# The second half of eight weight-row subtractions on GpSimd instead of VectorE, in a decoder layer on one core

## The chip, the cores and the metric

The kernel runs on one core of a Trainium2 chip. A core has TensorE (PE in the rows; PEld is its weight load), VectorE (DVE), ScalarE (ACT), GpSimd (POOL) and SyncE (SP), and 16 DMA engines; each compute engine works off its own queue in order, and the queues wait for each other through semaphores. The metric is the device time of the whole program in microseconds, measured without a profiler, as the median over runs.

## The reference

One decoder layer on 256 tokens of width 2048. What matters here is its beginning:

```python
c_act = jax.nn.silu(c)
mod = (c_act @ w_ada[l] + b_ada[l]).reshape(B, 6, 1, D)
shift1, scale1, gate1, shift2, scale2, gate2 = jnp.moveaxis(mod, 1, 0)
h = rmsnorm(x, g_norm_mix[l]) * (1.0 + scale1) + shift1
q_a, k_c, v_c, k_s, v_s, k_w, v_w, g_a, q_r, k_r, v_r, g_r = split_cols(h @ w_in[l], IN_SIZES)
...
x = x + gate1 * (jnp.concatenate([o_nsa, o_ret], axis=-1) @ w_out[l])
h2 = rmsnorm(x, g_norm_ffn[l]) * (1.0 + scale2) + shift2
x = x + gate2 * peer_ffn(h2, peer_w_q[l], peer_sub_keys[l], peer_u[l], peer_v[l])
```

The first projection `h @ w_in` feeds sparse attention and retention; the layer ends with a retrieval over 16384 single-neuron experts, whose two matrices of 128 MB each are streamed in whole.

## The kernel before, in words

Weights stay in float32. For a product at nearly float32 accuracy, a weight row is split into a high part `hi`, rounded to a narrower float32 form (`fp32r`) that TensorE takes, and a low part `lo = raw - hi`; activations are split in the same way into `hh` and `hl` (both in the tile `act`). A product is then three matmuls: hi·hh, hi·hl, lo·hh. `split_to` makes the two parts in two halves of the row: for each half a ScalarE copy (L157) makes `whi`, and a VectorE subtraction (L158) makes `wlo`.

The first projection runs in stages. Stage A, the one that the change touches, goes over `KH` = 8 rows of `winA`, k = 0 to 7, one row being the 128 inputs of block k by 2048 outputs. For each row:

- `win_row` loads 1 MB into one of four `raw` buffers (L348) and calls `split`.
- `row_in(k)` first makes two `ada_chunk`s per row: each loads a 1 MB row of `w_ada` into a `raw` buffer (L148) and multiplies and sums it against silu(c) with one VectorE `scalar_tensor_tensor` of 128x2048 (L198), whose sum is one column of scale1 or shift1. Two small VectorE operations (L338, L339) make `scol`, the scale of block k. Then `modulate` scales the block on ScalarE (L295, which needs `scol`), rounds it to `hh` on ScalarE (L296), and subtracts to `hl` on VectorE (L297).
- 48 matmuls of 128x256 (L354) go into the eight PSUM banks `bkA0` to `bkA7`.

So each row asks for 3 MB of DMA, and for two L158, two L198 and one L297 on VectorE. SyncE issues the loads in program order; a load waits until the buffer that it takes is free: of the three loads for block k+2, the first takes the buffer of `winA` row k, and so waits for both L158 of row k, and the next two take the buffers of the `ada` rows of block k+1, and wait for its two L198.

Ahead of the loop VectorE normalises the input with four products of 128x1024 (L300), after ScalarE has copied the row of inverse norms (`rrow`, L275); a 128x2 power on GpSimd (L221) stands in that chain. After the loop the eight banks are copied to `oT`, four on ScalarE (L372) and four on VectorE (L370), and stage C starts on `winC` with four of the banks.

The order on each engine is not that of the source: a list scheduler, which works with estimated durations, decides it when the program is built. Only loads and operations that are pinned keep the written order, and none in stage A is.

Of the kernel before, what the change touches and what calls it, by code (L numbers as in the profile page):

```python
# [9 lines left out]
F32 = mybir.dt.float32  # L10
# [105 lines left out]
def body(ctx, tc, a, out, dbg=None, stop=None):  # L116
    nc = tc.nc
# [15 lines left out]
    def chunk_tile(name, dt, tag=None):  # L133
        pool, bufs = strm[-1]
        return pool.tile([P, 2048], dt, name=name, tag=tag or name, bufs=bufs[tag or name])

    def raw_tile():
        if not ring:
            return chunk_tile("raw", F32)
        t = min(ring, key=lambda t: (ring[t][1] + 1) / ring[t][0])  # L140
        ring[t][1] += 1
        if t == "more":
            return ring[t][2].tile([P, 2048], F32, name="raw", tag="more", bufs=2)
        return chunk_tile("raw", F32, t)

    def load(src):
        r = raw_tile()
        i = nc.sync.dma_start(r, src)  # L148
        if ring:
            tc.keep_in_program_order(i)  # L150
        return r

    def split_to(r, hi, lo, parts=1):
        n = hi.shape[-1] // parts
        for i in range(parts):
            sl = slice(i * n, i * n + n)
            nc.scalar.copy(hi[:, sl], r[:, sl])  # L157
            nc.vector.tensor_sub(lo[:, sl], r[:, sl], hi[:, sl].bitcast(F32))  # L158

    def split(r, n=2048, parts=2):  # L160
        hi, lo = chunk_tile("whi", F32R)[:, 0:n], chunk_tile("wlo", F32R)[:, 0:n]
        split_to(r[:, 0:n], hi, lo, parts)
        return hi, lo


# [62 lines left out]
    def t_blocks(pool, src_chunks, tags=("A", "A"), parts=2, dst=None):  # L228

        if dst:  # L230
            split_to(load(src_chunks[0]), *dst, parts)
        w = [dst] if dst else [split(load(c), parts=parts) for c in src_chunks]
        ps = [pool.tile([P, 2, S], F32, name="psA", tag=t) for _, t in zip(w, tags)]
        for k in range(KB):
            sl = slice(k * P, (k + 1) * P)
            for p_, (hi, lo) in zip(ps, w):
                nc.tensor.matmul(p_, hi[:, sl], act[:, k], start=k == 0, stop=False, skip_group_check=True)  # L237
                nc.tensor.matmul(p_[:, 1, :], lo[:, sl], hh[:, k, :], start=False, stop=k == KB - 1, skip_group_check=True)  # L238
        return ps
# [39 lines left out]
    with ExitStack() as fctx:  # L279
# [48 lines left out]
        def background(n=1):  # L328
            credit[0] += PACE[n] if isinstance(n, str) else n
            n = int(credit[0] + 1e-6)  # L330
            credit[0] -= n
            for _ in range(n):
                if not todo:
                    return
                j, k = todo.pop(0)
                ada_chunk(j, k, crow)
                if j == 0:
                    nc.vector.tensor_add(modc[:, 0:2, k], modc[:, 0:2, k], b_col[:, 0:2, k])  # L338
                    nc.vector.tensor_scalar(scol[:, 0, k:k + 1], modc[:, 1, k:k + 1], 1.0, g_mix[:, k:k + 1],  # L339
                                            op0=OP.add, op1=OP.mult)  # L340
                elif 1 < j < 5 and k == KB - 1:
                    nc.vector.tensor_add(modc[:, j, :], modc[:, j, :], b_col[:, j, :])
                    if j == 4:
                        nc.vector.scalar_tensor_tensor(scol[:, 1, :], modc[:, 4, :], 1.0, g_ffn, op0=OP.add, op1=OP.mult)

        def win_row(src, k, n):
            r = raw_tile()
            nc.sync.dma_start(r[:, 0:n], src[k])  # L348
            return split(r, n)

        def rows_T(bank, b, hi, lo, col, k, k0, k1, first=True):
            w = slice(col, col + P)
            for n, (x, y) in enumerate(((hi, hh), (hi, hl), (lo, hh))):
                nc.tensor.matmul(bank[:, b, :], x[:, w], y[:, k, :], start=k == k0 and n == 0 and first,  # L354
                                 stop=k == k1 - 1 and n == 2, skip_group_check=True)
# [6 lines left out]
        def row_in(k):  # L362
            while len(todo) > 80 + LATE - 2 * (k + 1):
                background(1)
            modulate(k, k + 1, xT[:, k:k + 1, :], 0, 0, hh, hl)
# [8 lines left out]
        background(2)  # L374
        bk = banks("bkA", [P, 2, S], "AASSTTOO")
        for k in range(KH):
            hi, lo = win_row(a["winA"], k, 2048)
            row_in(k)
            background("A")
            for b in range(16):  # L380
                rows_T(bk[b // 2], b % 2, hi, lo, b * P, k, 0, KH, b % 2 == 0)
        wait_in(oT, bk)
        bk = banks("bkC", [P, 2, S], "AASS")
        for q in range(KH // 2):
            hi, lo = split(load(a["winC"][q].rearrange("p k e -> p (k e)")))
            background("C")
            for k in (2 * q, 2 * q + 1):
                for b in range(8):
                    rows_T(bk[b // 2], b % 2, hi, lo, (k % 2) * 1024 + b * P, k, 0, KH, b % 2 == 0)
# [4 lines left out]
        for k in range(KB):  # L394
            hi, lo = win_row(a["winB"], k, NB)
            if k >= KH:
                row_in(k)
            if len(todo) > 46 + LATE:
                background("B")
            for b in range(8):  # L400
                rows_T(bk[b // 2], b % 2, hi, lo, b * P, k, 0, KB, b % 2 == 0)
            for tt in range(2):
                ts_ = slice(tt * P, (tt + 1) * P)
                w = slice(8 * P, 8 * P + 512)
                for n, (x, y) in enumerate(((hh, hi), (hh, lo), (hl, hi))):
                    nc.tensor.matmul(bv[tt], x[:, k, ts_], y[:, w], start=k == 0 and n == 0,  # L406
                                     stop=k == KB - 1 and n == 2)
            rows_T(bg, 0, hi, lo, 8 * P + 512, k, 0, KB)
# [67 lines left out]
        for kv in range(2):  # L476
# [9 lines left out]
            for pb in range(16):  # L486
                i = nc.tensor.matmul(psc, w1[:, pb * P:(pb + 1) * P], blk[:, pb], start=pb == 0, stop=pb == 15)
# [34 lines left out]
        for gp in range(2):  # L522
# [91 lines left out]
            for q in range(2):  # L614
                src = []
# [89 lines left out]
        for q in range(4):  # L705
            sl = slice(q * 512, (q + 1) * 512)
# [20 lines left out]
        for q in range(4):  # L727
            sl = slice(q * 512, (q + 1) * 512)
# [613 lines left out]
def build(tc, a, out, dbg=None):  # L1342
    with ExitStack() as ctx:
        body(ctx, tc, a, out, dbg)
# [17 lines left out]
```

## Time and profile before

| what | value |
|---|---|
| median of 3 runs | 1859.46 us (1855.84 to 1864.89) |
| the profiled execution, its own time | 1856.91 us |
| its span | 1855.2 us |
| PE busy | 1793.1 us (97%) |
| VectorE busy | 1485.7 us (80%) |
| ScalarE busy | 708.7 us (38%) |
| GpSimd busy | 366.1 us (20%) |
| DMA | 653.96 MB, mean 353 GB/s |

Busy shares are means over the whole span. The stage that the change touches is the first 90 us, and what bounds the kernel there is read from rows of that stretch. Times in rows count from the start of the span.

### The profile page before, as it was taken

Reading aid. Unit: us, or ns where it says so; the run is one execution under the profiler, and the core shown is the slowest. Engines: PE = TensorE matmul, PEld = TensorE weight load, DVE = VectorE, ACT = ScalarE, POOL = GpSimd, SP = SyncE. Lnnn points to the kernel's source line nnn. Section 1 sums busy time; section 2 is a strip of 40 time slices with the busy share of each in tenths; the row PEclk is TensorE's granted clock in tenths of the full one; section 3 lists DMA queues with packets and bytes.
Section 4 is the critical chain, followed back from the end, with each engine's and each line's share of the span. In section 5 each row is a group of like instructions: output and inputs, shape, how many; then the busy total and the mean of one; then the engine's idle time right before and its main releaser. Section 6 shows DMA issues by size and latency. Waiting matters only on the chain.

```text
span 1855.2 us, 28510 instructions
## 1 busy us (share of the span) xinstructions
PE 1793.1 (97%) x11264; PEld 1571.5 (85%) x11264; DVE 1485.7 (80%) x2336; ACT 708.7 (38%) x1284; POOL 366.1 (20%) x259
## 2 busy tenths in 40 slices
PE   5899999999889999999999999999999999999997
PEld 4899878797767899999997777779999998777775
DVE  7988889889779999586498999983555558998878
ACT  3444453745435421021045555541111114555554
POOL 1000001011010012211124434420111114544210
PEclk9999899999999999999999999999999999999999
DMA  8989887889887799999889999989999989999992
GB/s 341 409 320 362 313 308 292 342 302 334 318 338 279 278 322 364 424 366 376 332 346 386 423 420 416 409 355 425 367 345 359 354 316 404 426 421 403 388 316 99
DMA packets 94616, 653.96 MB, mean 353 GB/s; under 512 B 11409, under 2 KB 11633, under 8 KB 18449
## 3 DMA queue, kind: packets, MB, share of 16 engines
q1 hardware_dynamic: 66818, 467.78, 65.2%
q0 software_dynamic: 27664, 184.37, 25.3%
q8 instruction: 88, 1.44, 0.3%
q14 instruction: 46, 0.38, 0.1%
HBM read 644.97 MB, written 4.22 MB: 350 GB/s over the span
## 4 chain that ended last, share of the span: by engine, by line
PE 87%; DVE 7%; DMA 3%; issue 1%; ACT 1%; POOL 0%; SPq 0%; ACTq 0%; POOLq 0%; DVEq 0%
PE acc L990 31%; PE psU L1111 28%; PE psN L453 8%; PE psD L354 4%; PE psA L237 3%; PE bkB L354 2%; DMA raw<-in_adaT 2%; PE psA L238 1%; PE pg L1096 1%; DVE raw L198 1%; DVE wlo L158 1%; PE bkC L354 1%; PE bvB L406 1%; DMA raw<-in_winA 1%; PE pT L552 1%
## 5 line engine op out<-in xcount | busy, mean ns | idle before, releaser
L1111 PE MATMUL psU<-xT,raw 128*128 128x160 f32 x4096 | 569.5, 300 | 0.0
L1111 PEld LDWEIGHTS psU<-xT,raw 128*128 128x128 f32 x4096 | 558.3, 190 | 0.4
L990 PE MATMUL acc<-whi,cc 128*128 128x512 f32 x1512 | 369.1, 391 | 0.0
L990 PEld LDWEIGHTS acc<-whi,cc 128*128 128x128 f32 x1512 | 283.8, 188 | 70.0 <-issue 1.5
L967 DVE TENSOR_TENSOR wlo<-raw,whi 128x2048 fp32r<-128x2048 f32 x126 | 288.1, 2287 | 55.1 <-issue 47.4
L990 PE MATMUL acc<-wlo,cc 128*128 128x512 f32 x1008 | 254.2, 392 | 0.8 <-DVE wlo L967 0.6
L964 ACT CAST whi<-raw 128x2048 fp32r<-128x2048 f32 x126 | 240.7, 1911 | 0.5 <-DMA raw<-in_v 0.5
L198 DVE SCALAR_TENSOR_TENSOR raw<-raw,crow 128x2048 f32<-128x2048 f32 x96 | 219.0, 2283 | 19.7 <-DMA raw<-in_adaT 19.6
L157 ACT CAST whi<-raw 128x1024 fp32r<-128x1024 f32 (+1 forms) x174 | 168.5, 1018 | 167.1 <-DMA raw<-in_winA 32.4
L158 DVE TENSOR_TENSOR wlo<-raw,whi 128x1024 fp32r<-128x1024 f32 (+1 forms) x174 | 200.6, 1181 | 24.2 <-ACT whi L157 23.8
L990 PEld LDWEIGHTS acc<-wlo,cc 128*128 128x128 f32 x1008 | 161.5, 161 | 63.8 <-DVE wlo L967 3.1
L453 PE MATMUL psN<-whi,act 128*128 128x512 f32 x512 | 166.9, 402 | 1.4 <-ACT act L677 0.7
L1117 DVE TENSOR_TENSOR X<-X,ge 128x160 f32<-128x160 f32 (+19 forms) x94 | 25.8, 276 | 162.7 <-ACT ge L1116 160.5
L1113 ACT ACTIVATE X<-psU 128x160 f32<-128x160 f32 (+19 forms) x102 | 25.6, 251 | 315.6 <-PE psU L1111 299.6
L453 PEld LDWEIGHTS psN<-whi,act 128*128 128x128 f32 x512 | 95.9, 189 | 25.6 <-issue 1.7
L453 PE MATMUL psN<-wlo,act 128*128 128x512 f32 x256 | 103.3, 404 | 3.4 <-DVE wlo L158 3.4
L953 ACT CAST cc<-X 128x192 fp32r<-128x192 f32 x126 | 44.0, 352 | 148.1 <-PE acc L990 147.5
L237 PE MATMUL psA<-act,whi 128*128 128x512 f32 x240 | 87.2, 404 | 3.8 <-ACT whi L157 3.8
L806 POOL DMA_INDIRECT rows<-in_urow,sx x32 | 67.1, 2097 | 105.3 <-DVE rows L847 100.4
L806 POOL DMA_INDIRECT s<-in_urow,sx x26 | 53.9, 2072 | 120.6 <-DVE s L847 86.5
L354 PE MATMUL psD<-act,whi 128*128 128x256 f32 x384 | 75.4, 294 | 0.6 <-ACT whi L157 0.6
L969 ACT CAST cc<-cc 128x64 fp32r<-128x64 f32 x126 | 30.4, 243 | 117.2 <-DVE cc L954 117.2
(363 smaller groups left out, 2551.0 us busy)
## 6 DMA issues: line engine op xcount, KB each, us to landing
raw<-in_u SPq DMA_DIRECT2D x128, 1024.0 KB
raw<-in_v SPq DMA_DIRECT2D x128, 1024.0 KB
raw<-in_adaT SPq DMA_DIRECT2D x96, 1024.0 KB
raw<-in_winN SPq DMA_DIRECT2D x16, 1024.0 KB
raw<-in_woutN SPq DMA_DIRECT2D x16, 1024.0 KB
raw<-in_wqT SPq DMA_DIRECT2D x16, 1024.0 KB
raw<-in_winB SPq DMA_DIRECT2D x16, 832.0 KB
raw<-in_winD SPq DMA_DIRECT2D x12, 1024.0 KB
```

The lines of the kernel that those rows point to most:

```text
L157: nc.scalar.copy(hi[:, sl], r[:, sl])
L158: nc.vector.tensor_sub(lo[:, sl], r[:, sl], hi[:, sl].bitcast(F32))
L198: nc.vector.scalar_tensor_tensor(r, r, 1.0, crow, op0=OP.mult, op1=OP.mult, accum_out=modc[:, j, k:k + 1])
L237: nc.tensor.matmul(p_, hi[:, sl], act[:, k], start=k == 0, stop=False, skip_group_check=True)
L354: nc.tensor.matmul(bank[:, b, :], x[:, w], y[:, k, :], start=k == k0 and n == 0 and first, stop=k == k1 - 1 and n == 2, skip_group_check=True)
L453: nc.tensor.matmul(ps[tt], x[:, k, ts_], y[:, w], start=k == 0 and j == 0, stop=k == KB - 1 and j == 2)
L806: pin(nc.gpsimd.indirect_dma_start(out=r, out_offset=None, in_=src, in_offset=bass.IndirectOffsetOnAxis(ap=o, axis=0)))
L953: inorder(nc.scalar.copy(ch, xb(j)))
L964: inorder(nc.scalar.copy(hi, r))
L967: nc.vector.tensor_sub(lo[:, i:i + n], r[:, i:i + n], hi[:, i:i + n].bitcast(F32))
L990: return nc.tensor.matmul(acc[c][0:m], x, w[:, c[1] * 512:(c[1] + 1) * 512], start=jj == 0 and n == 0, stop=jj == HALF - 1 and n == 2 - c[ ...
L1111: nc.tensor.matmul(ps, w[:, k * P:(k + 1) * P], xT[:, k, 0:TU], start=k == 0, stop=k == KB - 1)
```

## The change

The subtraction of the second half of each of the eight rows of stage A is given to GpSimd. Other callers of `split` and `split_to` keep VectorE.

```diff
-    def split_to(r, hi, lo, parts=1):
+    def split_to(r, hi, lo, parts=1, last=None):
         n = hi.shape[-1] // parts
         for i in range(parts):
             sl = slice(i * n, i * n + n)
             nc.scalar.copy(hi[:, sl], r[:, sl])
-            nc.vector.tensor_sub(lo[:, sl], r[:, sl], hi[:, sl].bitcast(F32))
-
-    def split(r, n=2048, parts=2):
+            (last if last and i == parts - 1 else nc.vector).tensor_sub(lo[:, sl], r[:, sl], hi[:, sl].bitcast(F32))
+
+    def split(r, n=2048, parts=2, last=None):
         hi, lo = chunk_tile("whi", F32R)[:, 0:n], chunk_tile("wlo", F32R)[:, 0:n]
-        split_to(r[:, 0:n], hi, lo, parts)
+        split_to(r[:, 0:n], hi, lo, parts, last)
         return hi, lo
...
-        def win_row(src, k, n):
+        def win_row(src, k, n, last=None):
             r = raw_tile()
             nc.sync.dma_start(r[:, 0:n], src[k])
-            return split(r, n)
+            return split(r, n, last=last)
...
         for k in range(KH):
-            hi, lo = win_row(a["winA"], k, 2048)
+            hi, lo = win_row(a["winA"], k, 2048, nc.gpsimd)
             row_in(k)
```

The scheduler sets a new order around the moved operations. On VectorE, before, the work from row 4 of `winA` (buffer `raw_468`) to row 5 (`raw_535`), with the two `ada` rows of block 5 (`raw_479`, `raw_482`) between:

```order
L158 TENSOR_TENSOR wlo_471<-raw_468,whi_470 128x1024 x2
L198 SCALAR_TENSOR_TENSOR raw_479,modc_65<-raw_479,crow_95 128x2048
L297 TENSOR_TENSOR act_70<-xT_60,act_70 128x256
L198 SCALAR_TENSOR_TENSOR raw_482,modc_65<-raw_482,crow_95 128x2048
L338 TENSOR_TENSOR modc_65<-modc_65,cols_58 128x2
L339 TENSOR_SCALAR scol_66<-modc_65,cols_58 128x1
```

And the same place on VectorE in the changed kernel:

```order
L158 TENSOR_TENSOR wlo_471<-raw_468,whi_470 128x1024
L297 TENSOR_TENSOR act_70<-xT_60,act_70 128x256
L198 SCALAR_TENSOR_TENSOR raw_479,modc_65<-raw_479,crow_95 128x2048
L198 SCALAR_TENSOR_TENSOR raw_482,modc_65<-raw_482,crow_95 128x2048
L338 TENSOR_TENSOR modc_65<-modc_65,cols_58 128x2
```

One of the two L158 is gone, and L297 has moved ahead of both L198. On ScalarE, before, the casts of rows 4 and 5 (`whi_470`, `whi_537`) and the scaling and rounding of blocks 4 and 5:

```order
L157 CAST whi_470<-raw_468 128x1024 x2
L295 ACTIVATE xT_60<-xT_60,modc_65,scol_66 128x256
L296 CAST act_70<-xT_60 128x256
L157 CAST whi_537<-raw_535 128x1024 x2
L295 ACTIVATE xT_60<-xT_60,modc_65,scol_66 128x256
L296 CAST act_70<-xT_60 128x256
```

And the same place on ScalarE in the changed kernel:

```order
L295 ACTIVATE xT_60<-xT_60,modc_65,scol_66 128x256
L157 CAST whi_470<-raw_468 128x1024 x2
L296 CAST act_70<-xT_60 128x256
L295 ACTIVATE xT_60<-xT_60,modc_65,scol_66 128x256
L157 CAST whi_537<-raw_535 128x1024 x2
L296 CAST act_70<-xT_60 128x256
```

L295 of a block, which waits for its `scol`, now stands ahead of the casts of the weight row of the same number; the casts stood ahead of it. At the end of stage A on ScalarE, before, the copies of four banks and the first row of `winC` (`whi_750`):

```order
L372 COPY oT_90<-bkA2_194 128x512
L157 CAST whi_750<-raw_748 128x1024 x2
L372 COPY oT_90<-bkA4_196 128x512
L295 ACTIVATE xT_60<-xT_60,modc_65,scol_66 128x256
L372 COPY oT_90<-bkA6_198 128x512
```

And in the changed kernel:

```order
L372 COPY oT_90<-bkA2_194 128x512
L372 COPY oT_90<-bkA4_196 128x512
L372 COPY oT_90<-bkA6_198 128x512
L157 CAST whi_750<-raw_748 128x1024 x2
L295 ACTIVATE xT_60<-xT_60,modc_65,scol_66 128x256
```

The casts of the first `winC` row now stand behind all four copies. GpSimd has the eight subtractions between the power of the input norm and the transfers of `kT`, and nothing else between these two; the order of SyncE's loads is the same in both kernels.

## Rows read from the trace of the kernel before

**Rows 1.** Windows: busy us per engine, clock, DMA share, GB/s.

```profile
50.00:60.00 10.00, 8.54 (x73) 8.33 (x72) 9.79 (x12) 4.31 (x7) 0.00 (x0) 1.00 1.01 412
70.00:80.00 10.00, 9.95 (x69) 9.75 (x70) 9.86 (x13) 3.33 (x5) 0.00 (x0) 0.83 0.99 399
90.00:100.00 10.00, 10.00 (x87) 10.00 (x86) 10.00 (x11) 5.85 (x9) 0.00 (x0) 1.00 0.86 329
...
68.00:70.00 2.00, 0.20 (x2) 0.00 (x0) 2.00 (x4) 0.00 (x0) 0.00 (x0) 1.00 1.04 438
72.00:74.00 2.00, 2.00 (x12) 2.00 (x11) 1.93 (x6) 1.97 (x4) 0.00 (x0) 0.50 0.93 381
```

**Rows 2.** Chain that ended last, rows 5 to 7: start, us, what.

```profile
56.72 7.19 DMA raw<-in_winA
63.99 1.06 ACT whi L157
65.08 2.36 DVE wlo L158 x2
67.44 2.21 DVE raw L198 x2
69.65 0.34 DVE act L297
69.99 2.22 DVE raw L198 x2
...
85.23 0.35 DVE act L297
85.62 5.00 PE bkA L354 x40
90.62 22.77 PE bkC L354 x192
```

**Rows 3.** Timeline of VectorE: start, us, operation, count.

```profile
22.52 2.35 DVE L158 TENSOR_TENSOR wlo<-raw,whi 128x1024 fp32r<-128x1024 f32 x2
24.79 4.63 DVE L300 TENSOR_TENSOR xT<-xT,rrow 128x1024 f32<-128x1024 f32 x4
...
41.51 0.21 DVE L339 TENSOR_SCALAR scol<-modc,cols 128x1 f32<-128x1 f32 x1
...
72.43 0.21 DVE L339 TENSOR_SCALAR scol<-modc,cols 128x1 f32<-128x1 f32 x1
```

**Rows 4.** Timeline of ScalarE, with the wait before and its releaser.

```profile
23.91 0.37 ACT L275 COPY rrow<-psr 128x256 f32<-128x256 f32 x1 [1.31 <-PE psr L271]
...
71.43 1.99 ACT L157 CAST whi<-raw 128x1024 fp32r<-128x1024 f32 x2 [4.49 <-DMA raw<-in_winA]
73.33 0.60 ACT L295 ACTIVATE xT<-xT,modc,scol 128x256 f32<-128x256 f32 x1
73.95 0.41 ACT L296 CAST act<-xT 128x256 fp32r<-128x256 f32 x1
...
88.19 1.99 ACT L157 CAST whi<-raw 128x1024 fp32r<-128x1024 f32 x2
```

**Rows 5.** GpSimd's 128x2 powers: all eight (min/median/max), then one beside VectorE.

```profile
L221 POOL TENSOR_TENSOR brs<-brs,mhalf x8: 685/1280/2832, 402.1 to 465.1; 128x2 f32<-128x2 f32 x8
...
445.85 1.51 POOL L221 TENSOR_TENSOR brs<-brs,mhalf 128x2 f32<-128x2 f32 x1 [14.47 <-ACT sg L633]
...
445.59 1.22 DVE L158 TENSOR_TENSOR wlo<-raw,whi 128x1024 fp32r<-128x1024 f32 x1
446.73 0.69 DVE L678 TENSOR_TENSOR act<-oT,act 128x512 fp32r<-128x512 f32 x1
```

**Rows 6.** Timeline of GpSimd: two memsets, and its first work after stage A.

```profile
2.66 0.99 POOL L472 MEMSET BD<- 128x1024 f32 x1
3.55 0.56 POOL L474 MEMSET hpad<- 128x512 f32 x1
...
185.83 2.50 POOL L418 DMA_DIRECT2D kT<-kcv  x4 [163.75 <-ACT kcv L410]
```

## The prediction

> **What bounds the kernel now.** I read the windows first. In stage A, from 50 to 80 us, VectorE is busy 9.8 of every 10 us and the 16 DMA engines are at a share of 0.99 to 1.01, while PE has gaps; from 90 us on PE is busy 10.00 of 10 [rows 1]. So stage A is paced by VectorE and the loads together, and what follows by PE. A delay of stage A's last matmul therefore moves the end by the same amount, since behind it PE has no idle time in which to catch up.
>
> Then the chain that ended last [rows 2]. The reader is to see one loop over two rows: a load of `winA` (7.2 us from issue to landing, because two `ada` loads are in flight ahead of it), 1.06 us of cast on ScalarE, 2.36 us for the two L158, 2.21 for the first L198, 0.34 for L297, 2.22 for the second L198, and the next load is issued. It leaves stage A at 85.58 us with the last L297, after which PE has 5.00 us of matmuls, and goes straight on into stage C at 90.62. The period follows from the operation that closes a block, L339 (`scol`): block 2's ends at 41.72 and block 6's at 72.64 [rows 3], 30.92 us for four rows, 7.73 each.
>
> Last, the timeline of ScalarE: it sits idle for 4.49 us for the weights, casts, and only then runs L295, whose `scol` was ready meanwhile [rows 4]. So before, casting waits for DMA and for nothing else, and `scol` of the next block is made on VectorE behind the subtractions.
>
> **The change, part by part.** *Removed from VectorE*: eight L158 of 1.18 us (half of 2.35 or 2.36), 9.4 us in all [rows 2, 3].
>
> *Added to GpSimd*: eight two-input subtractions of 128x1024. No row shows one. Below, a memset of that size takes 0.99 us, one stream out and none in. For the rate, 1024 columns against 512 cost 0.43 us more [rows 6], so one stream of 1024 is 0.85 us. For the fixed part, the power of 445.85 ends at 447.36, 0.55 us after VectorE's subtraction beside it (446.81) [rows 5]. Two inputs read one after the other make 0.55 + 2 × 0.85 = 2.25; with the output serial too, 3.1. I take G = 2.3 us, and keep 0.99 and 3.1 for the range. The Trainium skill, page "GPSIMD Engine Reference", section 3.1, measures 4497 ns for a float32 addition of 2048 columns, from which half would be an estimated 2.25 us; the sum by it would be 0.4 us lower. Nothing is queued behind the subtractions on GpSimd until 185.83 [rows 6].
>
> *Who holds whom.* Of the eight 128x2 powers, equal in shape, the shortest takes 0.69 us and the longest 2.83; the one shown starts while a VectorE subtraction runs and ends 0.55 us after it [rows 5]. GpSimd was held until that two-input operation was over, and got in at the boundary though VectorE had more queued. I read this as one resource with one holder, so that VectorE must wait in return when GpSimd holds it for a whole 1024-column read. No row shows that return: the L678 of 446.73 took its 0.69 us although the power ended within it, but a power reads two columns only. The Trainium skill says on page "SBUF — State Buffer", section "SBUF: two separate sides", that a VectorE operation with two SBUF inputs and a GpSimd operation that reads SBUF exclude each other for the whole instruction. By that rule the sum stays as below; the trace agrees for GpSimd's side (2.83 against 0.69 us), and the power that ended inside L678 speaks against "whole". If only the trace's side were true, the first rival's time would hold.
>
> *Moved.* The new order makes it worse. L295 of a block stands ahead of the casts of its row, so the casts now wait for `scol`. And L297 stands ahead of both L198. Counted from the end of `scol`: L295 0.60 and a handoff of 0.05; first cast until VectorE subtracts, 1.06; L158, 1.18: 2.89 us. The second cast is over at 2.64, so GpSimd waits and gets in at 2.89; L297 is ready only at 3.05 (0.41 of L296 behind the casts [rows 4]), so GpSimd is first. Then G; L297 0.34; two L198, 4.43; L338 and L339, 0.43 (72.21 to 72.64 [rows 2, 3]). The period is 8.09 + G = 10.4 us, against 7.73. In it VectorE idles 1.7 us for ScalarE and 2.3 for GpSimd. Loads no longer pace: 3 MB took 7.7 us at the full share.
>
> *The sum.* Start: L300 begins at 23.69 + G instead of 24.79, +1.2; the second GpSimd operation comes due while the L300s run and holds VectorE behind them, +G, less the L158 that went, 1.18; together 2G − 2.28 = +2.3. Four periods to block 6: 4 × 10.39 − 30.92 = +10.6. From there to the last L297, 12.94 us before (72.64 to 85.58): now one period and 2.89 + G + 0.34, 15.92, so +3.0. Altogether 8G − 2.46 = +15.9.
>
> *Into stage C*: before, the first `winC` cast starts at 88.19, 2.4 us before PE leaves stage A [rows 2, 4], and costs nothing. Now it stands behind the copy of bank 6, which PE finishes some 0.6 us before its last matmul; a copy of 0.6 later ScalarE casts, so that PE waits 1.06 us for its first weight and about 0.3 more for the first low part: +1.4.
>
> 1856.91 + 15.9 + 1.4 = 1874.2 us. The profiled execution lies 2.6 us under the median of the three runs, so on their scale it would be 1876.8; I say 1875.
>
> *Left open*: PE's clock. PE was busy for 0.20 of the 2 us before 70, and then the granted clock was 0.50, its lower level of 1.2 GHz, in 72 to 74, with 12 matmuls in 2 us instead of about 20; a mean of 0.83 over 70 to 80 is 3.4 us at that level [rows 1], so 1.7 us of work lost. The new pauses are longer. Inside the rows this hides (PE has pauses there); behind the last L297 it would not. I leave it out of the sum and put it into the range.
>
> **Rivals.**
>
> *VectorE is not held* (15%). GpSimd subtracts beside it. L300 begins when the copy of `rrow` ends at 24.28 [rows 4], −0.5, and one L158 less, −1.2. L297 follows L296 at 3.1 us, so the period is 8.3: four make +2.3; the last stretch is 8.3 + 3.44, −1.2. With stage C's 1.4 that is +0.8: 1857.7 us, no difference that can be told. For it: L678's unchanged time. Against it: the powers' waits.
>
> *A short hold* (5%). VectorE is held, but G is under 1.3 us: 8G + 1855.9 gives 1863.8 at 0.99, and the limit of 0.5% is met at G = 1.3.
>
> *Faster: VectorE's relief reaches the end* (2%). The place is VectorE's row loop, the price 1.18 us a row, 9.4 in all, 1847.5 us. It decides if the weights still land later than `scol` is ready, so that L295 ahead of the casts costs nothing, and if loads leave room. Against it: the DMA share is 1.01 at 412 GB/s [rows 1], at which 3.15 MB take 7.6 us, so the period can fall by 0.1 only; with the start's 1.7 the gain is some 2 to 3 us, about 1854.5, unless the loads speed up too.
>
> **How the numbers follow.** VectorE held by a GpSimd operation of 1.3 to 3.1 us has 78%; its likeliest time is 1875, and its own range 1866 to 1883 (3.1 gives 1880.7, and 1.7 for the clock 1882.4). To leave out no more than 2 in 10 the range goes down to the unheld case: 1858 to 1883. What a measurement of this kernel can tell from no change is about 0.5%, 9.3 us: slower by more 0.78, within it 0.20 (not held, or a short hold), faster by more 0.02.
>
> **What would show it.** In the changed trace, eight L158 rows on GpSimd of about 2.3 us, longer where VectorE's L300 or L158 runs when they come due; VectorE's L297 starting only as GpSimd ends, in each row; L339 to L339 of 10.4 us; idle time of VectorE ahead of L158 put down to the cast; the last L297 near 101.5 us; a DMA share well under 1 in 50 to 100; and PE waiting about 1.4 us at the start of stage C. A period of 8.3 with L297 inside GpSimd's operation would mean no hold. I am wrong altogether if PE takes back the time behind 100 us, or if the order costs less because ScalarE's cast does not wait for `scol`.

## The result, and the profile after

The changed kernel takes 1876.36 us (median of 4 runs, 1874.77 to 1879.05), against 1859.24 before on the same chip: a ratio of 1.0089, 95% interval 1.0073 to 1.0105. It is slower by 17.1 us; 1875 was predicted. The profiled execution took 1879.05 us, with a span of 1877.3, against 1856.91 before: 22.1 us more, of which 6.5 arise only behind 480 us and have another origin (below).

The windows of the changed kernel, with the columns of [rows 1]:

```profile
50.00:60.00 10.00, 7.53 (x49) 7.12 (x49) 8.30 (x9) 2.79 (x4) 2.41 (x1) 0.84 0.81 310
70.00:80.00 10.00, 7.50 (x48) 7.10 (x47) 8.30 (x9) 2.79 (x4) 2.41 (x1) 0.83 0.86 316
...
102.00:104.00 2.00, 2.00 (x11) 2.00 (x11) 2.00 (x4) 0.58 (x1) 0.00 (x0) 0.50 0.96 401
```

In stage A the DMA share has fallen from 0.99 to 1.01 [rows 1] to 0.81 to 0.86, and VectorE reads 8.30 of 10 us busy instead of 9.79. That looks like relief, but a held operation counts as busy: 2 of the 8.30 us are waiting, as VectorE's timeline shows [rows 3]:

```profile
24.10 6.10 DVE L300 TENSOR_TENSOR xT<-xT,rrow 128x1024 f32<-128x1024 f32 x4 [0.59 <-ACT rrow L275]
30.12 2.56 DVE L297 TENSOR_TENSOR act<-xT,act 128x256 fp32r<-128x256 f32 x1
...
53.76 0.21 DVE L339 TENSOR_SCALAR scol<-modc,cols 128x1 f32<-128x1 f32 x1
55.58 1.23 DVE L158 TENSOR_TENSOR wlo<-raw,whi 128x1024 fp32r<-128x1024 f32 x1 [1.61 <-PE bkA L354]
56.83 2.48 DVE L297 TENSOR_TENSOR act<-xT,act 128x256 fp32r<-128x256 f32 x1
59.23 2.28 DVE L198 SCALAR_TENSOR_TENSOR raw<-raw,crow 128x2048 f32<-128x2048 f32 x1
...
63.97 0.21 DVE L339 TENSOR_SCALAR scol<-modc,cols 128x1 f32<-128x1 f32 x1
```

A row now takes 63.97 − 53.76 = 10.21 us from `scol` to `scol`, against 7.73. Two pieces of it are new: 1.61 us of idle time ahead of L158, and an L297 of 2.48 us that took 0.42 where GpSimd was idle (the row of 40.68). GpSimd, a group and then its timeline; the group gives min, median and max in ns:

```profile
L158 POOL TENSOR_TENSOR wlo<-raw,whi x8: 2403/2406/3260, 22.4 to 97.5; 128x1024 fp32r<-128x1024 f32 x8
...
22.45 3.26 POOL L158 TENSOR_TENSOR wlo<-raw,whi 128x1024 fp32r<-128x1024 f32 x1 [0.59 <-ACT whi L157]
29.85 2.54 POOL L158 TENSOR_TENSOR wlo<-raw,whi 128x1024 fp32r<-128x1024 f32 x1 [4.14 <-ACT whi L157]
56.62 2.41 POOL L158 TENSOR_TENSOR wlo<-raw,whi 128x1024 fp32r<-128x1024 f32 x1 [7.80 <-ACT whi L157]
```

GpSimd works from 56.62 to 59.03, and L297, begun at 56.83, is over only behind it, at 59.31. The 1.61 us are explained by ScalarE's timeline [rows 4], of a row and of the way into stage C:

```profile
54.01 0.60 ACT L295 ACTIVATE xT<-xT,modc,scol 128x256 f32<-128x256 f32 x1 [7.42 <-DVE scol L339]
54.52 1.98 ACT L157 CAST whi<-raw 128x1024 fp32r<-128x1024 f32 x2
56.40 0.40 ACT L296 CAST act<-xT 128x256 fp32r<-128x256 f32 x1
...
106.30 0.58 ACT L372 COPY oT<-bkA 128x512 f32<-128x512 f32 x1 [0.36 <-PE bkA L354]
106.78 2.00 ACT L157 CAST whi<-raw 128x1024 fp32r<-128x1024 f32 x2
```

Before, ScalarE waited 4.49 us for the weights [rows 4]; now it waits 7.42 for `scol`, with L295 at the head of its queue and the casts behind it. (The row above puts the wait of 1.61 us down to PE, other rows put the same 1.61 us down to the cast; in all six rows L158 starts 1.06 or 1.07 us behind the start of the first cast, so it is the cast.) The chain that ended last [rows 2] has taken both in:

```profile
54.52 1.98 ACT whi L157 x2
56.87 2.37 issue
59.23 4.51 DVE raw L198 x4
...
97.68 2.49 DVE act L297
100.21 6.06 PE bkA L354 x36
107.86 1.24 DVE wlo L158
109.14 22.04 PE bkC L354 x184
...
483.79 6.12 DMA raw<-in_adaT
494.60 10.01 DMA raw<-in_adaT
```

The loads of `winA` are gone from it. The 2.37 us called "issue" are the hold: L297 had started and waited for nothing that the profile knows of. Up to the end of stage C the balance closes. The last L297 ends at 100.16 instead of 85.58 (14.6). What follows is read from PE's timeline, of the changed kernel:

```profile
106.45 0.28 PE L354 MATMUL bkA<-act,wlo 128*128 128x256 f32 x1
107.88 1.21 PE L354 MATMUL bkC<-act,whi 128*128 128x256 f32 x8 [1.15 <-ACT whi L157]
```

and of before:

```profile
90.46 1.11 PE L354 MATMUL bkC<-act,whi 128*128 128x256 f32 x8
91.41 0.33 PE L354 MATMUL bkC<-act,wlo 128*128 128x256 f32 x1
```

From the first of the last 40 matmuls of stage A to the first of stage C it was 4.84 us (85.62 [rows 2] to 90.46), and now it is 7.67 (100.21 to 107.88). The chain's 6.06 us hold only 36 of the 40. The last one starts at 106.45, and matmuls start 0.12 us apart there, so without a pause stage C would have begun near 106.6. So 1.5 us are lost because the granted clock was 0.50 (1.2 GHz) in 102 to 104 after PE's pauses in the rows, and 1.3 us because PE waits for the cast. The first matmul with a low part comes 1.26 us behind the first of stage C (109.14 − 107.88) instead of 0.95 (91.41 − 90.46), which makes 0.3. With a rest of 0.1 these are 17.8 us, and stage B's first matmul (`bkB`) starts at 131.02 instead of 113.23.

### The profile page after: what moved, and what is told of

Same layout as the page of the kernel before. It is cut to its first block, busy times and chain, and to the rows that moved or that the text cites. A ratio compares the mean times of both kernels' runs of the same rounds, so it can differ in the third digit from the quotient of the medians.

```text
span 1877.3 us, 28537 instructions
## 1 busy us (share of the span) xinstructions
PE 1802.6 (96%) x11264; PEld 1578.6 (84%) x11264; DVE 1492.8 (80%) x2328; ACT 708.8 (38%) x1284; POOL 386.2 (21%) x267
## 4 chain that ended last, share of the span: by engine, by line
PE 81%; DVE 9%; DMA 4%; issue 4%; ACT 2%; POOL 0%; SPq 0%; POOLq 0%; ACTq 0%; DVEq 0%
PE acc L990 28%; PE psU L1111 27%; PE psN L453 8%; PE psA L237 3%; PE bkB L354 2%; PE psD L354 2%; DVE raw L198 2%; DMA raw<-in_adaT 2%; DMA rows<-in_v,sx 2%; PE psA L238 1%; PE pg L1096 1%; PE bkC L354 1%; PE bvB L406 1%; DVE wlo L158 1%; ACT whi L157 1%
## 5 line engine op out<-in xcount | busy, mean ns | idle before, releaser
L198 DVE SCALAR_TENSOR_TENSOR raw<-raw,crow 128x2048 f32<-128x2048 f32 x96 | 218.6, 2282 | 22.3 <-DMA raw<-in_adaT 22.1
L158 DVE TENSOR_TENSOR wlo<-raw,whi 128x1024 fp32r<-128x1024 f32 (+1 forms) x166 | 191.7, 1179 | 34.1 <-ACT whi L157 27.6
L354 PE MATMUL bkA<-act,whi 128*128 128x256 f32 x256 | 58.7, 327 | 22.1 <-ACT act L296 11.2
L806 POOL DMA_INDIRECT rows<-in_v,sx x25 | 63.0, 2522 | 57.3 <-DVE sp L853 31.3
```

The lines of the kernel that those rows point to most:

```text
L158: (last if last and i == parts - 1 else nc.vector).tensor_sub(lo[:, sl], r[:, sl], hi[:, sl].bitcast(F32))
L198: nc.vector.scalar_tensor_tensor(r, r, 1.0, crow, op0=OP.mult, op1=OP.mult, accum_out=modc[:, j, k:k + 1])
L806: pin(nc.gpsimd.indirect_dma_start(out=r, out_offset=None, in_=src, in_offset=bass.IndirectOffsetOnAxis(ap=o, axis=0)))
```

## The experiments

Two ways were used to keep the order of instructions in hand. In the first four and in the ninth, tenth and twelfth, only stage A's rows 2 to 7 are pinned to an order; the scheduler may then choose another order behind stage A. In the others the place of every instruction of every engine is written out, so that nothing but the named change moves. The period, the end of the last L297 and the start of stage B (first `bkB` matmul) are from the profile; the times are medians over all runs of a kernel. Before took 1860.21 us beside the first four, 1859.05 beside the fifth to eighth, 1860.26 beside the ninth and 1859.56 beside the eleventh:

| kernel | period, us | last L297 ends | stage B starts | median, us | ratio to before (95%) |
|---|---|---|---|---|---|
| before | 7.73 | 85.58 | 113.23 | 1859.24 | |
| changed | 10.21 | 100.16 | 131.02 | 1876.36 | 1.0089 (1.0073 to 1.0105) |
| 1 order alone, stage A | 9.17 | 91.60 | 121.54 | 1863.66 | 1.0017 (1.0008 to 1.0026) |
| 2 hold alone, stage A | 8.54 | 92.62 | 121.74 | 1869.65 | 1.0047 (1.0033 to 1.0060) |
| 3 GpSimd copies | 8.88 | 92.36 | 122.90 | 1868.30 | 1.0042 (1.0027 to 1.0057) |
| 4 GpSimd only writes | 8.15 | 88.12 | 118.08 | 1866.18 | 1.0025 (1.0012 to 1.0038) |
| 5 order alone, whole | 9.17 | 91.84 | 121.79 | 1870.07 | 1.0054 (1.0034 to 1.0073) |
| 6 hold alone, whole | 8.61 | 92.83 | 120.50 | 1868.01 | 1.0039 (1.0023 to 1.0056) |
| 7 entry as before, whole | 10.21 | 100.22 | 130.21 | 1874.68 | 1.0079 (1.0064 to 1.0095) |
| 8 L300 later, whole | 7.86 | 83.07 | 110.74 | 1856.86 | 0.9985 (0.9973 to 0.9997) |
| 9 quarter on GpSimd | 9.73 | 99.69 | 128.79 | 1878.35 | 1.0097 (1.0079 to 1.0116) |
| 11 quarter, whole | 9.73 | 96.39 | 126.35 | 1875.59 | 1.0082 (1.0068 to 1.0096) |

### Order or hold: experiments 1, 2, 5 and 6

The theory is that of the prediction: GpSimd's subtraction holds VectorE, and the new order costs by itself. The rivals are that one of the two is the whole of it. In the first, a row of stage A was written in the changed kernel's order, with VectorE for the second half:

```diff
-            second = lambda: sub(nc.gpsimd, c1)
+            second = lambda: sub(nc.vector, c1)
```

> The changed kernel's new order in stage A (L295 ahead of the casts, L297 ahead of both L198), but VectorE subtracts the second half again. Theory, that the order and GpSimd's hold on VectorE both cost: the period from scol to scol is 1.61 us (VectorE idle until the first cast is over) + 2.36 (two L158) + 0.4 (L297) + 4.42 (two L198) + 0.5, about 9.3 us, between the 7.73 of before and the 10.21 of the change; the last L297 ends near 92.6 us; about 1866 us. Rival, that the new order explains the whole loss: a period of 10.2 us and 1876 us. Rival, that the hold explains it all: a period of 7.7 us and 1859 us.

In the second, the calls of a row were put in the order of before, with GpSimd kept (`rest` is L297, `background(1)` one `ada` row, `scale` is L295):

```diff
-            scale()
             cast(c0)
+            sub(nc.vector, c0)
             cast(c1)
             second()
+            scale()
...
-                background(2)
+                background(1)
+                rest()
+                background(1)
```

> The order of before in stage A (casts ahead of L295, L297 between the two L198), but GpSimd subtracts the second half. Theory, that the order and the hold both cost: the period is 1.18 us (one L158) + about 2.2 of hold + 4.42 (two L198) + 0.34 (L297) + 0.5, about 8.7 us; about 1866 to 1867 us. Rival, that the order explains the whole loss: 7.7 us and 1858 to 1859 us. Rival, that the hold explains it all: 10.2 us and 1876 us.

Stage A came out as the theory has it: periods of 9.17 (9.3 expected) and 8.54 us (8.7), the last L297 6.0 and 7.0 us late. The times did not: the second lies 3 us above the 1866 to 1867 expected, and the first only 3.5 us over before, where stage A lost 6. Behind stage A its order is not that of either kernel, so its time can't be laid to stage A alone. Hence the same two again, with every instruction's place written out. The fifth is the changed kernel's order on VectorE, with the second half back in it:

```diff
 L158 TENSOR_TENSOR wlo<-raw,whi 128x1024
+L158 TENSOR_TENSOR wlo<-raw,whi 128x1024
 L297 TENSOR_TENSOR act<-xT,act 128x256
 L198 SCALAR_TENSOR_TENSOR raw,modc<-raw,crow 128x2048
```

> Every engine's order is that of the changed kernel from the first to the last instruction, written out, and VectorE does the eight second halves again, each right behind its first half; nothing else differs from the changed kernel. Theory, that the new order costs a period of 9.17 us (as in the first experiment) and the entry into stage C: the last L297 ends 6 us later than before, stage C 8 to 9 us later, and the time is about 1868 us. Rival, that the first experiment's small loss of 3 us is the order's real price: about 1863 us. Rival, that the order explains the whole loss: 1876 us.

The sixth is the order of before, with the second half taken out and given to GpSimd:

```diff
 L158 TENSOR_TENSOR wlo<-raw,whi 128x1024
-L158 TENSOR_TENSOR wlo<-raw,whi 128x1024
 L198 SCALAR_TENSOR_TENSOR raw,modc<-raw,crow 128x2048
 L297 TENSOR_TENSOR act<-xT,act 128x256
```

> Every engine's order is that of the kernel before from the first to the last instruction, written out, and the eight second halves stand on GpSimd; nothing else differs from the kernel before. Theory, that GpSimd's hold costs about 0.8 us a row of the period (8.55 against 7.73, as in the second experiment): the last L297 ends 7 us later than before, stage C is entered without a pause, and the time is about 1867 to 1868 us. Rival, that the hold explains the whole loss: 1876 us. Rival, that the hold costs nothing by itself: 1860 us.

By the medians the order alone costs 11.0 us (1870.07 against 1859.05 on the same chip) and the hold alone 9.0, with intervals that overlap; which of the two is dearer can't be told from them. VectorE in the fifth:

```profile
52.46 2.36 DVE L158 TENSOR_TENSOR wlo<-raw,whi 128x1024 fp32r<-128x1024 f32 x2 [1.60 <-ACT whi L157]
54.74 0.42 DVE L297 TENSOR_TENSOR act<-xT,act 128x256 fp32r<-128x256 f32 x1
```

and in the sixth:

```profile
60.90 1.22 DVE L158 TENSOR_TENSOR wlo<-raw,whi 128x1024 fp32r<-128x1024 f32 x1
63.03 3.48 DVE L198 SCALAR_TENSOR_TENSOR raw<-raw,crow 128x2048 f32<-128x2048 f32 x1 [0.91 <-DMA raw<-in_adaT]
```

In the fifth the 1.60 us of idle time stay and L297 is back to 0.42. In the sixth there is no idle time for a cast, and now L198 is held: 3.48 us instead of 2.28. Its hold is cheaper than L297's because part of it falls into 0.91 us in which the `ada` row is not there yet. By the start of stage B the order costs 8.6 us, the hold 7.3 and both 17.8: 2 us more than the sum. That would fit a hold that hides behind loads where the order is the old one, but was not tried by itself. At a later place, GpSimd's eighth power on `brs` (shown below), the order has cost 8.3 us, the hold 5.8 and both 15.6. Neither alone explains the loss, and both rivals fall.

### What holds VectorE: experiments 3, 4, 10 and 12

> The changed kernel's order; GpSimd's subtraction in rows 2 to 7 is a copy with one input (the second half of the low part becomes a copy of the high part, so the low product of half the columns is left out). Theory, that VectorE is held for as long as GpSimd's operation lasts and that each input adds a read of its own: GpSimd takes about 0.55 + 0.85 = 1.4 us, L297 takes about 1.5 us, the period is about 9.2 us, the time about 1867 us. Rival, that only a two-input operation of GpSimd holds VectorE: L297 takes 0.4 us, the period is 8.3 us and the time about 1858 us. Rival, that the hold does not follow GpSimd's duration: L297 stays at 2.5 us and the time at 1876 us.

```diff
-            second = lambda: sub(nc.gpsimd, c1)
+            second = lambda: nc.gpsimd.tensor_copy(lo[:, c1], hi[:, c1].bitcast(F32))
```

> The changed kernel's order; in place of the subtraction GpSimd copies 128x2 (so that it waits for the second cast as before) and then writes the second half of the low part of rows 2 to 7 with a constant of zero, so that no wide operand is read (the low product of half the columns is left out). Theory, that it is GpSimd's reading that holds VectorE: L297 ends during the memset and takes 0.4 to 0.9 us, the period is about 8.3 to 8.5 us and the time 1858 to 1860 us. Rival, that any work of GpSimd holds VectorE: L297 ends with the memset and takes 1.0 us or more, the period is about 9 us and the time about 1866 us.

```diff
-            second = lambda: sub(nc.gpsimd, c1)
+            second = lambda: (nc.gpsimd.tensor_copy(tick, hi[:, 2046:2048].bitcast(F32)), nc.gpsimd.memset(lo[:, c1].bitcast(F32), 0.0))
```

The timelines of a row of the third, and of the fourth:

```profile
55.48 1.09 POOL L396 CAST wlo<-whi 128x1024 fp32r<-128x1024 f32 x1 [7.78 <-ACT whi L393]
55.70 1.15 DVE L395 TENSOR_TENSOR act<-xT,act 128x256 fp32r<-128x256 f32 x1
```

```profile
55.04 0.95 POOL L398 MEMSET wlo<- 128x1024 f32 x1
55.09 0.42 DVE L397 TENSOR_TENSOR act<-xT,act 128x256 fp32r<-128x256 f32 x1
```

L297 (L395 and L397 here) takes 1.15 us beside a GpSimd copy of 1.09, and 0.42 beside a memset of 0.95. So the hold follows the time of a GpSimd operation that reads, and a pure write holds nothing. The theory's price of the copy, 1.4 us, was too high; the third's period of 8.88 us and its 1868.30 are near the 9.2 and 1867 that it gave. The fourth's period of 8.15 us is what the new order costs with one L158 fewer on VectorE and no hold, close to the 8.3 of the prediction's first rival. Its time is 6 us over before's, and not the 1858 to 1860 that was expected: 2.5 us are stage A's, and 2.3 more are there by the start of stage B (118.08 against 113.23), of which 1.3 are two pauses of PE at the entry into stage C (1.03 and 0.30 us). Where the rest of the 6 arises was not followed.

The tenth puts a VectorE operation with one operand beside GpSimd's subtraction, and the twelfth a sum:

```diff
+            one = lambda: nc.vector.tensor_copy(scr, r[:, 0:256]) if k % 2 else nc.vector.tensor_scalar(scr, r[:, 0:256], 2.0, None, op0=OP.mult)
...
             second()
+            one()
             nc.scalar.copy(hh[:, k, :], t)
             rest()
+            one()
```

> The changed kernel's order in stage A, with two extra VectorE operations of 128x256 in rows 2 to 7 that read one operand (a copy in odd rows, a multiplication by a constant in even rows; their result is not used): one between L158 and L297, where GpSimd is subtracting, and the same again behind L297, where it is not. Theory, that VectorE is held only when it reads two operands itself: the first one takes as long as the second (0.2 to 0.4 us) and runs beside GpSimd's subtraction, and L297 behind it still ends with GpSimd. Rival, that any VectorE work is held: the first one ends with GpSimd and takes about 2.2 us more than the second, and L297 takes its 0.4 us.

```diff
-            one = lambda: nc.vector.tensor_copy(scr, r[:, 0:256]) if k % 2 else nc.vector.tensor_scalar(scr, r[:, 0:256], 2.0, None, op0=OP.mult)
+            one = lambda: nc.vector.reduce_sum(scr[:, 0:1], r[:, 0:256], axis=mybir.AxisListType.X)
```

> As the tenth experiment, but the two extra VectorE operations of each row are sums over 256 columns (128x256 to 128x1, result not used) in place of the copy or multiplication. In the tenth, a copy of 128x256 took 0.28 us outside GpSimd's subtraction and 2.46 beside it. Theory, that only an operation that reads at more than one element a cycle, by one or two operands, is held (a copy of 256 columns took 0.28 us, L297 with two operands 0.42): a sum, at one element a cycle, takes as long beside GpSimd's subtraction as behind it (0.3 to 0.5 us), and L297 behind it is held instead, so the period stays near 10.2 to 10.6 us. Rival, that any VectorE operation on SBUF is held: the first sum takes about 2.2 us more than the second, and L297 its 0.42 us.

VectorE in the tenth, GpSimd at work from 57.41 to 59.81, and in the twelfth, GpSimd from 56.79 to 59.19:

```profile
57.50 2.46 DVE L399 COPY scr<-raw 128x256 f32<-128x256 f32 x1
59.88 0.41 DVE L397 TENSOR_TENSOR act<-xT,act 128x256 fp32r<-128x256 f32 x1
60.22 0.28 DVE L399 COPY scr<-raw 128x256 f32<-128x256 f32 x1
```

```profile
56.88 0.41 DVE L399 TENSOR_REDUCE scr<-raw 128x1 f32<-128x256 f32 x1
57.21 2.26 DVE L397 TENSOR_TENSOR act<-xT,act 128x256 fp32r<-128x256 f32 x1
59.40 0.41 DVE L399 TENSOR_REDUCE scr<-raw 128x1 f32<-128x256 f32 x1
```

The copy is held though it reads one operand: 2.46 us beside GpSimd, 0.28 alone, and the same for the multiplication in the even rows. The tenth's theory, that only two operands matter, falls. The sum, which takes 0.41 us for 256 columns instead of 0.28, is not held at all, and the L297 behind it is. That fits the twelfth's theory and ends its rival, that any operation is held. But a sum also writes one column where the copy writes 256, and no run separates the two. The twelfth's period is 10.53 us, the tenth's 10.61. One execution each, with the extra work in it, took 1881.95 and 1883.23 us. The Trainium skill, page "SBUF — State Buffer", section "SBUF: two separate sides", names an operation of VectorE in a two-port mode, or one with two SBUF inputs against a GpSimd operation that reads SBUF, as what excludes GpSimd; the traces agree on the copy (2.46 against 0.28), on L297 (2.48 against 0.42) and on the memset (0.42).

### The entry into stage C: experiment 7

The changed kernel, every place written out, with the casts back in their place of before on ScalarE; on VectorE the first L158 of that row stands ahead of the last bank copy again, and the second right behind it:

```diff
 L372 COPY oT<-bkA2 128x512
+L157 CAST whi<-raw 128x1024 x2
 L372 COPY oT<-bkA4 128x512
 L372 COPY oT<-bkA6 128x512
-L157 CAST whi<-raw 128x1024 x2
```

> The changed kernel with every order written out, but at the entry into stage C the casts of the first row of winC stand ahead of the copies of banks 4 and 6 again, and its subtractions ahead of VectorE's last bank copy, as in the kernel before. Theory, that this place costs PE 2.1 us: PE enters stage C without its pause, and the time falls by about 2 us against the change, to about 1874.3 us. Rival, that the row or VectorE is late there anyway: no difference, 1876.4 us.

Its PE, the first of the last 40 matmuls of stage A and the way into stage C:

```profile
100.28 0.58 PE L354 MATMUL bkA<-act,whi 128*128 128x256 f32 x1 [0.73 <-DVE act L297]
...
107.20 1.11 PE L354 MATMUL bkC<-act,whi 128*128 128x256 f32 x8
108.33 0.39 PE L354 MATMUL bkC<-act,wlo 128*128 128x256 f32 x1
```

The cast starts at 104.37 instead of 106.78, and PE goes from `bkA` to `bkC` without a pause. But stage B starts 0.8 us earlier only, not 2.1: the last 40 matmuls of stage A take 6.9 us instead of 6.4, at a granted clock of 0.50 (1.2 GHz) from 100 to 104, where the changed kernel had 0.68 and 0.50. In the times the difference to the changed kernel is 1.7 us, with intervals that overlap, and by GpSimd's eighth power on `brs` nothing of it is left (480.74 against 480.67). The pause is shown; that the way out of it is worth 2 us is not.

### How much goes by columns: experiments 9 and 11

```diff
-            second = lambda: sub(nc.gpsimd, c1)
+            second = lambda: (sub(nc.gpsimd, slice(1536, 2048)), sub(nc.vector, slice(1024, 1536)))
```

> The changed kernel's order in stage A, but GpSimd subtracts only the last 512 columns of rows 2 to 7 and VectorE the 512 before them. VectorE gets back 0.59 us of the 1.18 a row. Theory, that a subtraction on GpSimd has a fixed part of 0.55 us and a part by columns (0.55 + 1.85 at 1024): it takes 1.48 us, the period is 10.21 + 0.59 - 0.92, about 9.9 us, the time about 1874.5 us. Rival, that its cost goes by columns alone: 1.20 us, a period of 9.6 us and about 1873 us. By both it stays slower than the kernel before (7.73 us a row).

GpSimd in the ninth, min, median and max in ns:

```profile
L394 POOL TENSOR_TENSOR wlo<-raw,whi x6: 1317/1324/1329, 46.6 to 95.3; 128x512 fp32r<-128x512 f32 x6
```

512 columns take 1.32 us and 1024 take 2.41, so 1.08 goes with every 512 columns and about 0.24 is fixed: between the two answers, nearer to the rival, and a period of 9.73 us. Stage B starts 2.2 us earlier than in the changed kernel (one L198 of 2.28 us stands ahead of the last L297 here, hence its 99.69), but the time did not fall: a ratio of 1.0097 against 1.0089, with intervals that overlap. Whether that is the order behind stage A was asked by the eleventh:

> The changed kernel with every engine's order written out from the first to the last instruction, but in all eight rows GpSimd subtracts only the last 512 columns, and VectorE the 512 before them, right behind its first half. Theory, that the ninth experiment's stage A (a period of 9.73 us against 10.21) was hidden in its time by another order behind stage A: with the changed kernel's order there, stage A ends about 3.5 us earlier than in the changed kernel and the time is about 1873 us. Rival, that a smaller share on GpSimd gains nothing in the end: 1876 to 1878 us.

With the changed kernel's order, stage B starts 4.7 us earlier than there, and the median is 1875.59, 0.8 us lower, with runs from 1869.01 to 1877.59. So the theory's 1873 is not shown by the median. The trace shows the gain: at GpSimd's eighth power on `brs` the eleventh is 3.7 us ahead of the changed kernel (477.01 against 480.67). Its profiled execution took 1869.01 us, 10 less than that of the changed kernel; the section on the prediction has one reason for such spreads.

### A version that beats both: experiment 8

Two of the four L300 (blocks 8 to 15) are moved from the head of stage A to VectorE's pause in stage C, where before it waited 2.92 us for a cast; L295 to L297 of block 8 follow them. VectorE's order:

```diff
-L300 TENSOR_TENSOR xT<-xT,rrow 128x1024 x4
+L300 TENSOR_TENSOR xT<-xT,rrow 128x1024 x2
...
 L158 TENSOR_TENSOR wlo<-raw,whi 128x1024 x2
+L300 TENSOR_TENSOR xT<-xT,rrow 128x1024 x2
 L158 TENSOR_TENSOR wlo<-raw,whi 128x1024 x2
```

> The kernel before with every order written out, but two of the four L300 (blocks 8 to 15, 2.3 us of VectorE) moved from the head of stage A into VectorE's pause in stage C, with block 8's L295 to L297 behind them. Theory, that stage A is paced by VectorE: it ends up to 2.3 us earlier and the time is about 1858 us against 1860. Rival, that the loads pace it as well (a DMA share of 1.01): no difference, or under 1 us.

Its VectorE at the two places, and its chain:

```profile
24.49 2.35 DVE L300 TENSOR_TENSOR xT<-xT,rrow 128x1024 f32<-128x1024 f32 x2
...
97.21 2.35 DVE L300 TENSOR_TENSOR xT<-xT,rrow 128x1024 f32<-128x1024 f32 x2
```

```profile
83.13 5.00 PE bkA L354 x40
88.13 22.78 PE bkC L354 x192
```

PE leaves stage A 2.5 us earlier (88.13 against 90.62), 2.4 of them are still there at GpSimd's eighth power on `brs`, and the median is 1856.86 us against 1859.05: 2.2 us faster, with an interval that just excludes no change.

## Why the prediction was right

*GpSimd's time* (G = 2.3): 2.41 us measured. The value is right, its make-up is not: 0.55 fixed and 0.85 for each input would make a copy 1.4 us, and it took 1.09; half the columns took 1.32, which leaves 0.24 as fixed.

*Who holds whom*: right, in both directions. No row of before showed VectorE's side; L297 beside GpSimd takes 2.48 to 2.56 us instead of 0.42, in seven of eight rows. And GpSimd is held too: its eight subtractions take 2.40 to 3.26 us by their records, but each ends 2.19 to 2.24 us behind the end of the L158 or L300 during which it came due (59.03 behind 56.81, for one). The first rival (not held) is out, and so is the short hold, as G is above 1.3. Why L678 of before was not held by the power in [rows 5] was not tried; the power reads two columns.

*The new order*: right, and about as dear as the hold: 8.6 us alone by the start of stage B, the hold 7.3; 11.0 and 9.0 by the medians, which can't rank them.

*The sum*: 15.9 us predicted up to the last L297, 14.6 measured. By its parts: start +2.3, measured 2.0 (`scol` of block 2 at 43.55 instead of 41.51); four periods +10.6, measured 9.9; last stretch +3.0, measured 2.6. The step that is off is the constant 8.09 of the period: it laid L158, GpSimd and L297 end to end. In the trace GpSimd starts 0.19 us before L158's record ends, and L198 follows 0.20 behind GpSimd's end, not 0.34. With the measured G the formula would have given 10.50, not 10.21.

*Into stage C*: +1.4 predicted, 1.6 measured (1.3 for the cast, 0.3 for the low part); the place and the cause were right.

*The clock*: left out of the sum, and put into the range with 1.7 us. It cost 1.5. So a sum 1.3 too high was met by terms 1.8 too low, and that 17.3 stands beside 17.8 by the start of stage B is luck in the sizes, not in the mechanism. The step from 1876.8 down to 1875 was given no reason.

*No way back behind 100 us*: right on the whole. GpSimd's eighth power on `brs`, of before:

```profile
465.08 0.71 POOL L221 TENSOR_TENSOR brs<-brs,mhalf 128x2 f32<-128x2 f32 x1 [6.20 <-DVE brs L663]
```

and of the changed kernel:

```profile
480.67 0.71 POOL L221 TENSOR_TENSOR brs<-brs,mhalf 128x2 f32<-128x2 f32 x1 [7.02 <-DVE brs L663]
```

It comes 15.6 us later, so 2.2 us were gained back from the start of stage B (349.65 against 351.85). From there to the end of the span the changed kernel took 1396.6 us and before 1390.1. The sum knows nothing of these 6.5 us. Of them 4.9 lie in two loads. Of the changed kernel these stand at the end of the chain above, 6.12 and 10.01 us; the chain of the fifth experiment, which has the same order, has

```profile
476.45 4.89 DMA raw<-in_adaT
...
486.03 6.32 DMA raw<-in_adaT
```

Before has 4.87 and 6.39, and the sixth experiment, with before's order, 6.27 and 9.89. So the same two loads, queued in the same order, take 11.2 or 16.1 us, in either order; before was profiled in the short case and the changed kernel in the long one. The other 1.6 us follow behind the loads, where PE's granted clock was 0.50 and 0.63 from 505 to 515, against 0.77 and 0.89 from 485 to 495 in before. In before, the changed kernel and the five kernels with every place written out, the stretch from the eighth power to the end takes 1389.4 to 1390.1 us with the short loads (five kernels) and 1396.6 or 1396.8 with the long ones (two). So the change itself has cost 15.6 us by that place, and the 17.1 of the medians, so near to the predicted 17.3, may hold a share of long loads. What decides between the two cases stays open, and so does how much of the spread of the times comes from it.

*The other signs*: the DMA share fell as predicted; GpSimd's first two operations are the longer ones (3.26 and 2.54 us), where VectorE's L158 and L300 ran. That L297 would start only as GpSimd ends came in another form: its record starts beside GpSimd's and ends behind it.

## What to carry to other kernels

An idle GpSimd is not spare VectorE: before moving work there, ask whether the GpSimd operation reads SBUF, and whether what VectorE does meanwhile can be held by it. Here 1.18 us of VectorE work became 2.41 of GpSimd's, of which VectorE waited 2.06. Price the order that a scheduler makes of a moved instruction as a term of its own, and when testing it, write out the whole program's order, since a partly pinned one moves other stages too (1863.66 against 1870.07 for the same stage A). When executions differ by something that the change does not touch, compare traces at a place ahead of it. Where a stage is paced by an engine, look for work in it that a later stage has a pause for.

## What was not expected of the hardware

A VectorE copy of 256 columns with a single operand waits GpSimd's subtraction out (2.46 us against 0.28), which the tenth's theory had ruled out, while a sum over the same columns runs beside it at its full speed (0.41 us both ways). GpSimd's copy of 128x1024 took 1.09 us, where 1.4 was expected, less than half of its two-operand subtraction (2.41) and little more than a memset (0.95). Two loads of 1 MB took 11.2 us together in some executions and 16.1 in others, with nothing changed in the order around them.
